# Padding the on-chip tiles of a four-layer decoder trunk so that matmul operands begin at multiples of 128 bytes

## The chip, the cores and the metric

The kernel runs on one core of one Trainium2 chip. The metric is device time in microseconds, the median of several runs. The profile is of one execution on that core, taken by the hardware profiler.

## What is computed

The reference is a small decoder trunk on 512 tokens of width 1024 in float32, with two layers. Each layer adds to the residual stream x: half a SwiGLU block, a token mixer, and half a second SwiGLU block, each behind an RMS norm.

```python
for layer in range(DEPTH):                      # 2
    x = x + 0.5 * _swiglu(_rmsnorm(x, g[0]), w_gate0, w_up0, w_down0)
    h = _rmsnorm(x, g[1])
    mix = _conv_rwkv_mixer(h, ...) if layer % 2 == 0 else _mla_mixer(h, ...)
    x = x + mix
    x = x + 0.5 * _swiglu(_rmsnorm(x, g[2]), w_gate1, w_up1, w_down1)

def _swiglu(h, w_gate, w_up, w_down):           # 1024 -> 2816 -> 1024
    return (jax.nn.silu(h @ w_gate) * (h @ w_up)) @ w_down
```

So there are four SwiGLU blocks. The mixer of layer 0 is a gated short convolution beside an RWKV-7 recurrence, that of layer 1 latent attention with 8 heads. Most of the arithmetic is in the four SwiGLU blocks.

## The kernel before

Activations are kept transposed: channels on the 128 partitions, the 512 tokens along the free axis, so x is eight tiles x0 to x7 of 128x512 float32. Products in float32 are made from two halves: a value is split into a rounded part ("h", type fp32r) and what is left ("l"), and the helper `mm3` (L98 to L102) issues three matmuls into one PSUM tile: weight-h by x-h (L100), weight-h by x-l (L101), weight-l by x-h (L102). In each the x operand is streamed (512 columns), and a 128x128 block of weights is loaded ahead of it as the stationary operand.

`weight` (L64) brings 128x512 float32 of weights by one DMA into a ring of four raw tiles (wr), ACT makes the rounded half (wh, L71), DVE or GpSimd the rest (wl, L72), in rings of four each. `gemm_steps` (L82) walks the contraction in blocks of 128 and calls mm3 for each.

`ffn` (L158) is one SwiGLU block. For each of 22 column blocks it accumulates a gate tile pg and an up tile pu over the eight x tiles (48 matmuls: three into pg, three into pu, and so on): this is called the gate/up phase here, 22 x 48 = 1056 matmuls. DVE and ACT make the activation of each block in temporary tiles and split it into ah and al, which stay on chip. Then for each of eight output blocks po is accumulated over the 22 ah/al tiles: the down phase, 8 x 66 = 528 matmuls. In both phases TensorE takes its instructions in the order written; other engines follow through semaphores that the framework sets.

The layers between use the same mm3 for their larger products (pp and po in layer 0; po in layer 1). Layer 1 has more split products written out in place: pab (L400 to L402, 384 and 320 columns), pq and pk (L556 to L558, 384 and 512 columns; here the weights are streamed and the tile ch or cl of a token block is stationary), the scores ps (L603 to L607, key tiles kh and kl streamed, query tiles stationary) and attention times values (L642 to L644). L608 adds the mask to the scores by a short bf16 matmul.

Where a tile lies: each pool gives its tiles consecutive places in every partition, each rounded up to 32 bytes, and a pool begins where the one opened before it ends. The first tile of the kernel lies at a multiple of 128. From the sizes in the code this gives, modulo 128 bytes:

```
tiles                                   before           after
raw and split weights wr, wh, wl          96               0
x, split x (xh, xl), oh, ol               96               0
temporary tiles, six buffers      96,0,32,64,96,0          0
ah, al                                    32               0
layer 0: large tiles (mb, b, ar, ma)       0               0
layer 0: tiles of g()              0, 32, 64, 96           0
layer 1: split input weights wih, wil     96               0
layer 1: ch, cl of token block 0..3   0,32,64,64     64,96,0,0
layer 1: q, k, v of head pairs 0, 2       96               0
layer 1: q, k, v of head pairs 1, 3        0               0
layer 1: th, tl                            0               0
```

The columns of a weight tile that one matmul loads begin a multiple of 512 bytes further in; only the first two projections of layer 0, with 64 and 96 columns a block, step by 256 and 384 bytes.

Of the kernel before, what the change touches and what calls it, by code (L numbers as in the profile page):

```python
# [8 lines left out]
F32 = mybir.dt.float32  # L9
# [8 lines left out]
WCOL = 512  # L18
NRAW = 4
NSPLIT = 4  # L20


class Lazy:
    def __init__(self, make):
        self.make = make
# [5 lines left out]
class Trunk:  # L31
    def __init__(self, tc, d, stack):
        self.tc, self.nc, self.d = tc, tc.nc, d
        nc = self.nc
        open_ = lambda **k: stack.enter_context(tc.tile_pool(**k))
        self.cp = open_(name="const", bufs=1)
        self.wp = open_(name="w", bufs=3)
        self.xp = open_(name="xs", bufs=1)
        self.tp = open_(name="tmp", bufs=6)
        self.mm = open_(name="mm", bufs=4, space=PSUM)  # L40
        self.sm = open_(name="sm", bufs=4, space=PSUM)
        self.n = 0
        self.filler = iter(())
        self.x = [self.xp.tile([128, T], F32, name=f"x{k}") for k in range(KD)]
        self.xh = self.xl = None
        self.gains = self.cp.tile([128, 6, KD], F32, name="gains")
        nc.sync.dma_start(self.gains, d["gains"])
        self.loaded = 0
        self.load(0)
        self.ones = self.cp.tile([128, 128], F32, name="ones")  # L50
        nc.vector.memset(self.ones, 1.0)
        self.eps = self.cp.tile([128, 1], F32, name="eps")
        nc.vector.memset(self.eps, 1e-6)
        warm = self.cp.tile([128, 1], F32, name="warm")
        nc.scalar.activation(warm, self.eps, AF.Silu)

    def uid(self, s):
        self.n += 1
        return f"{s}_{self.n}"

    def t(self, name, n=T, dt=F32, p=128):
        return self.tp.tile([128, 520], dt, name=self.uid(name), tag="t")[0:p, 0:n]

    def weight(self, src, cols, scale=None, lo_on=None):  # L64
        nc = self.nc
        raw = self.wp.tile([128, WCOL], F32, name=self.uid("wr"), tag="wr", bufs=NRAW)[:, 0:cols]
        hi = self.wp.tile([128, WCOL], F32R, name=self.uid("wh"), tag="wh", bufs=NSPLIT)[:, 0:cols]
        lo = self.wp.tile([128, WCOL], F32R, name=self.uid("wl"), tag="wl", bufs=NSPLIT)[:, 0:cols]
        nc.sync.dma_start(raw, src)
# [10 lines left out]
            pass  # L80

    def gemm_steps(self, outs, nk, m, xh, xl, lo_on=None):  # L82
        """outs: [(psum, weight block [128, nk * m])]; contraction over nk tiles of x."""
        step = min(nk, WCOL // m)
        for k0 in range(0, nk, step):
            k1 = min(nk, k0 + step)
            w = [self.weight(src[:, k0 * m : k1 * m], (k1 - k0) * m, lo_on=lo_on) for _, src in outs]
            for k in range(k0, k1):
                s = slice((k - k0) * m, (k - k0 + 1) * m)
                for (ps, _), (wh, wl) in zip(outs, w):  # L90
                    self.mm3(ps, wh[:, s], wl[:, s], xh[k], xl[k], k == 0, k == nk - 1)
                    yield
# [109 lines left out]
class Mla(Trunk):  # L202
# [136 lines left out]

    def qkv(self, pool):  # L340
        t = lambda n, a, b: pool.tile([128, a, b], F32R, name=self.uid(n), tag=n)
        sq = pool.tile([128, 8], F32, name=self.uid("sq"), tag="sq")
        return t("qh", 4, T), t("ql", 2, T), t("kh", 4, T), t("kl", 4, T), t("vh", 4, 256), t("vl", 4, 256), sq

    def mla_out(self, hp):
# [15 lines left out]
    def mla_in(self, iw, q0):  # L361
        nc, d = self.nc, self.d
        self.win = []
        for k in range(KD):
            h = iw.tile([128, 704], F32R, name=f"wih{k}")
            l = iw.tile([128, 704], F32R, name=f"wil{k}")
            for c in (slice(0, 384), slice(384, 704)):
                raw = self.wp.tile([128, WCOL], F32, name=self.uid("wr"), tag="wr", bufs=NRAW)[:, 0 : c.stop - c.start]
                nc.sync.dma_start(raw, d["w_oi"][k][:, c])
                nc.scalar.activation(h[:, c], raw, AF.Copy)  # L370
                (nc.vector if k % 2 == 0 else nc.gpsimd).tensor_tensor(l[:, c], raw, h[:, c], op=ALU.subtract)
            self.win.append((h, l))
        self.rt = self.mp.tile([128, 4], F32, name="rt")
        self.ch, self.cl, self.kr, self.kb = [], [], [], []
        self.cur, self.pab = self.qkv(q0), {}
        proj = self.mla_proj(0, self.cur)
        self.in_mm((0, 1))
        post = [self.in_post(iw, 0)]
        for tb in range(1, 4):
            if tb > 1:  # L380
                self.in_mm((tb,))
            post.append(self.in_post(iw, tb))
            self.in_t(post.pop(0))
            if tb >= 2:
                for _ in range(2):
                    next(proj)
        self.in_t(post.pop(0))
        return proj
# [260 lines left out]


DECAY = float(np.exp(-0.5))
# columns of the per-channel parameter block
MU_R, MU_K, MU_V, MU_L, MU_G, W0, A0, KK, KA, RK, LNW, LNB, CW = 0, 4, 8, 12, 13, 14, 18, 22, 26, 30, 34, 38, 42
NEV = 54
G = 520
LORA_FILL = 1
DECAY_FILL = 1
KEYS_FILL = 3
# [9 lines left out]
class Even(Mla):  # L668
# [26 lines left out]
    def g(self, tag, n=T, p=128, dt=F32):  # L695
        bufs = 3 if tag == "c" else 1
        return self.gp.tile([128, G], dt, name=self.uid(tag), tag=tag, bufs=bufs)[0:p, 0:n]

    def even_setup(self):
        nc, d, rp = self.nc, self.d, self.rp  # L700
        self.ev = rp.tile([128, NEV], F32, name="ev")
        nc.sync.dma_start(self.ev, d["ev"])
        self.om = rp.tile([128, 14], F32, name="om")
        nc.vector.tensor_scalar(self.om, self.ev[:, 0:14], -1.0, 1.0, op0=ALU.mult, op1=ALU.add)
        self.oka = rp.tile([128, 8], F32, name="oka")
        nc.vector.tensor_scalar(self.oka[:, 0:4], self.ev[:, KA : KA + 4], -1.0, None, op0=ALU.mult)
        nc.vector.tensor_scalar(self.oka[:, 4:8], self.ev[:, KA : KA + 4], 1.0, -1.0, op0=ALU.mult, op1=ALU.add)
        self.mask = rp.tile([128, 128], F32, name="emask")
        nc.sync.dma_start(self.mask, d["emask"])
        self.bones = rp.tile([128, 128], F32, name="bones")  # L710
        nc.sync.dma_start(self.bones, d["bones"])
        self.zero = rp.tile([128, 64], F32, name="zero")
        nc.gpsimd.memset(self.zero, 0.0)
        self.gneps = rp.tile([128, 1], F32, name="gneps")
        nc.vector.memset(self.gneps, 64e-5)
# [383 lines left out]
def lay_mla(inp,o):  # L1099
    a={k:np.asarray(v) for k,v in inp.items()}  # L1100
    c=np.ascontiguousarray
    o["ident"]=np.eye(128,dtype=np.float32)
    o["mask"]=np.triu(np.full((128,128),-1e30,np.float32),1)
    o["pos"]=c(a["positions"].reshape(4,128).T)
    fr=(10000.0**(-np.arange(0,64,2)/64)).astype(np.float32)
    o["freq"]=c(np.broadcast_to(fr.astype(np.float32),(128,32)))
    qn,kn=a["mla_q_norm"][0],a["mla_k_norm"][0]
    o["nope_g"]=c(np.broadcast_to(np.concatenate([qn[:128],kn[:128]]),(128,256)))
    o["rope_g"]=c(np.broadcast_to(np.concatenate([qn[128:],kn[128:]]),(128,128)))
    o["mla_v"]=c(np.concatenate([a["mla_q_a_norm"][0].reshape(3,128).T,a["mla_kv_a_norm"][0].reshape(2,128).T],1))  # L1110
    o["w_oi"]=c(a["odd_w_in"][0].reshape(8,128,704))
    w=a["mla_w_kv_up"][0].reshape(2,128,4,2,2,128)  # k p hp h (kn|v) d
    o["w_kv"]=c(w.transpose(2,1,0,4,3,5).reshape(4,128,1024))
    i=np.arange(192)
    w=a["mla_w_q_up"][0].reshape(3,128,4,384)[...,np.concatenate([i,192+(i+128)%192])]
    o["w_q"]=c(w.transpose(2,1,0,3).reshape(4,128,1152))
    w=a["odd_w_out"][0].reshape(4,2,128,8,128)  # hp c p m d
    o["w_oo"]=c(w.transpose(0,2,3,1,4).reshape(4,128,2048))
    return o

def lay_even(inp,o):
    a={k:np.asarray(v) for k,v in inp.items()}
    c=np.ascontiguousarray
    w=a["even_w_in"][0]  # [1024, 3232]: b 512 | c 512 | h 512 | r k v 512 | dw 32 da 32 dg 96
    rk=1536
    blocks=[w[:, rk+1536:rk+1600], w[:, rk+1600:rk+1696]]
    rwkv=lambda i,j: w[:, rk+i*512+j*128:rk+i*512+j*128+128]
# [3 lines left out]
    for j in range(4):  # L1131
        s=slice(j*128,j*128+128)
        b,cc,h=(w[:,i*512:i*512+512][:,s] for i in range(3))
# [4 lines left out]
    pad=lambda v:np.concatenate([v,np.zeros(128-len(v),np.float32)])[:,None]  # L1138
# [14 lines left out]
def layout(inp):  # L1153
    return lay_even(inp, lay_mla(inp, lay(inp)))
# [33 lines left out]
```

## Time and profile before

| what | value |
|---|---|
| median of 3 runs | 2049.99 us (2046.57 to 2051.52) |
| span of the profiled execution, from the first to the last instruction | 2044.8 us |
| the profiled execution's own time beside its span | not listed; the runs' times are 1.8 to 6.7 us over this span |
| TensorE busy | 96% of the span, 10030 matmuls |
| VectorE, ScalarE, GpSimd busy | 53%, 38%, 15% |
| DMA engines, mean busy share | 28%, 85 GB/s |
| gate/up phases | about 25 to 254, 734 to 962, 1097 to 1326, 1689 to 1918 us |
| down phases | 254 to 377, 962 to 1086, 1326 to 1449, 1918 to 2041 us |
| layer 0 mixer, layer 1 mixer | 377 to 717 us, 1449 to 1677 us |

How to read it: PE is the matmul part of TensorE, PEld its weight loads, which overlap the matmuls. Matmuls are pipelined: the start of the next comes before the end of the one before, so the durations of single matmuls overlap and their sum is more than the span. What a matmul costs in a long row of them is the distance from start to start, which can be had from a count in a stretch, or from first and last start of a group. [...]

### The profile page before, as it was taken

The numbers are of one execution on the slowest core, as the hardware profiler recorded it, in microseconds if no ns is written. First come the engines' busy times: TensorE is split into PE (matmuls) and PEld (weight loads), VectorE is DVE, ScalarE is ACT, GpSimd is POOL, SyncE is SP. The second block draws the span as 40 slices with busy tenths as digits, with TensorE's granted clock in tenths as the row PEclk, the third lists the DMA queues.
The fourth block names the chain that finished last, engine by engine and source line by source line (L and its number), as shares of the span: only waits on it lengthen the run. The fifth ranks groups of instructions, "written<-read, shape, count | busy, mean of one in ns | idle before, by whom it ended". The sixth has DMA issues, their size and how long they took to land.

```text
span 2044.8 us, 26989 instructions
## 1 busy us (share of the span) xinstructions
PE 1964.4 (96%) x10030; PEld 1590.4 (78%) x10030; DVE 1080.7 (53%) x1914; ACT 771.5 (38%) x1497; POOL 298.6 (15%) x342
## 2 busy tenths in 40 slices
PE   8999999967999999999999999999988999999999
PEld 6888888746776778888888888888877778888887
DVE  6444433499954864444335444433377775444422
ACT  5333332533422443333233333333475544333221
POOL 2000000266333410000000000000353430000000
PEclk9999999988999999999999999999998999999999
DMA  4333333221111123323332332333311123333332
GB/s 144 97 97 99 91 101 92 82 63 52 46 38 53 61 93 96 101 93 101 91 95 95 94 102 93 96 98 94 95 36 33 42 68 103 94 103 93 103 109 78
DMA packets 99892, 174.47 MB, mean 85 GB/s; under 512 B 11792, under 2 KB 20496, under 8 KB 99760
## 3 DMA queue, kind: packets, MB, share of 16 engines
q1 hardware_dynamic: 99760, 172.74, 28.1%
q8 instruction: 79, 1.29, 0.3%
q14 instruction: 53, 0.43, 0.1%
HBM read 170.60 MB, written 2.10 MB: 84 GB/s over the span
## 4 chain that ended last, share of the span: by engine, by line
PE 64%; DVE 8%; issue 3%; POOL 2%; ACT 1%; DMA 1%; POOLq 0%; SPq 0%; ACTq 0%; DVEq 0%
PE po L100 7%; PE po L101 7%; PE po L102 7%; PE pu L100 6%; PE pg L100 6%; PE pu L102 6%; PE pg L101 6%; PE pu L101 6%; PE pg L102 6%; PE pp L100 1%; PE pp L101 1%; PE pp L102 1%; PE s L907 0%; POOL s L493 0%; DVE pr L932 0%
## 5 line engine op out<-in xcount | busy, mean ns | idle before, releaser
L71 ACT ACTIVATE wh<-wr 128x512 fp32r<-128x512 f32 (+2 forms) x647 | 399.2, 619 | 919.5 <-PE pg L101 452.9
L72 DVE TENSOR_TENSOR wl<-wr,wh 128x512 fp32r<-128x512 f32 (+2 forms) x567 | 383.2, 679 | 428.0 <-ACT wh L71 427.5
L100 PE MATMUL pg<-xh,wh 128*128 128x512 f32 x704 | 277.2, 394 | 6.6 <-ACT wh L71 6.0
L100 PE MATMUL pu<-xh,wh 128*128 128x512 f32 x704 | 275.2, 391 | 3.2 <-DVE x L1085 2.6
L101 PE MATMUL pg<-xl,wh 128*128 128x512 f32 x704 | 275.5, 391 | 2.3 <-DVE xl L118 2.3
L102 PE MATMUL po<-ah,wl 128*128 128x512 f32 x704 | 277.4, 394 | 0.0
L100 PE MATMUL po<-ah,wh 128*128 128x512 f32 x704 | 277.4, 394 | 0.0
L101 PE MATMUL po<-al,wh 128*128 128x512 f32 x704 | 277.4, 394 | 0.0
L102 PE MATMUL pg<-xh,wl 128*128 128x512 f32 x704 | 275.0, 391 | 0.0
L102 PE MATMUL pu<-xh,wl 128*128 128x512 f32 x704 | 274.9, 391 | 0.0
L101 PE MATMUL pu<-xl,wh 128*128 128x512 f32 x704 | 274.8, 390 | 0.0
L173 DVE TENSOR_TENSOR g<-pg,rinv 128x512 f32<-128x512 f32 x88 | 60.9, 692 | 286.9 <-PE pg L102 286.5
L137 POOL TENSOR_TENSOR acc<-acc,sq 128x512 f32<-128x512 f32 x42 | 57.1, 1360 | 1061.6 <-ACT sq L136 1061.3
L100 PEld LDWEIGHTS pg<-xh,wh 128*128 128x128 f32 x704 | 132.8, 189 | 35.7 <-ACT wh L71 6.0
L100 PEld LDWEIGHTS pu<-xh,wh 128*128 128x128 f32 x704 | 132.7, 189 | 32.1 <-ACT sin L282 2.9
L101 PEld LDWEIGHTS pg<-xl,wh 128*128 128x128 f32 x704 | 132.9, 189 | 31.9 <-DVE xl L118 3.7
L102 PEld LDWEIGHTS po<-ah,wl 128*128 128x128 f32 x704 | 131.6, 187 | 32.7
L100 PEld LDWEIGHTS po<-ah,wh 128*128 128x128 f32 x704 | 131.7, 187 | 32.6
L101 PEld LDWEIGHTS po<-al,wh 128*128 128x128 f32 x704 | 131.7, 187 | 32.5
L102 PEld LDWEIGHTS pu<-xh,wl 128*128 128x128 f32 x704 | 132.6, 188 | 28.1 <-DVE wl L72 0.5
L102 PEld LDWEIGHTS pg<-xh,wl 128*128 128x128 f32 x704 | 132.8, 189 | 27.8 <-DVE wl L72 0.5
L101 PEld LDWEIGHTS pu<-xl,wh 128*128 128x128 f32 x704 | 132.7, 189 | 27.4
(365 smaller groups left out, 2633.8 us busy)
## 6 DMA issues: line engine op xcount, KB each, us to landing
wr<-in_wg SPq DMA_DIRECT2D x176, 256.0 KB, 2.6
wr<-in_wu SPq DMA_DIRECT2D x176, 256.0 KB, 2.9
wr<-in_wd SPq DMA_DIRECT2D x160, 256.0 KB, 2.7
wr<-in_w_ei SPq DMA_DIRECT2D x49, 256.0 KB, 2.7
wr<-in_wd SPq DMA_DIRECT2D x32, 128.0 KB, 2.1
wr<-in_w_eo SPq DMA_DIRECT2D x16, 256.0 KB, 2.7
wr<-in_w_oo SPq DMA_DIRECT2D x16, 256.0 KB, 3.1
wr<-in_w_q SPq DMA_DIRECT2D x12, 192.0 KB, 2.4
```

Of the source, the lines that this page charges most:

```text
L71: nc.scalar.activation(hi, raw, AF.Copy)
L72: (lo_on or nc.vector).tensor_tensor(lo, raw, hi, op=ALU.subtract)
L100: nc.tensor.matmul(ps, wh, xh, start=first, stop=False)
L101: nc.tensor.matmul(ps, wh, xl, start=False, stop=False)
L102: nc.tensor.matmul(ps, wl, xh, start=False, stop=last)
L137: nc.gpsimd.tensor_tensor(acc, acc, sq, op=ALU.add)
L173: nc.vector.tensor_tensor(g, pg, rinv, op=ALU.mult)
```

## The change

No instruction is added, removed or moved. Six tiles get longer or a tile that nobody uses is put behind others, so that what is allocated after them shifts: 32 bytes behind the constants (all later pools), the temporary tiles from 520 to 544 floats, the tiles of `g` in layer 0 from 520 to 544, the parameter block `ev` from 54 to 64 floats, `sq` from 8 and `rt` from 4 to 32 floats in layer 1. The column "after" in the table above is the outcome. The rest of the diff takes out comments.

```diff
+CONST_PAD = 8
+TMP = 544
@@ class Trunk: __init__
         nc.scalar.activation(warm, self.eps, AF.Silu)
+        self.cp.tile([128, CONST_PAD], F32, name="pad")
@@ def t
-        return self.tp.tile([128, 520], dt, name=self.uid(name), tag="t")[0:p, 0:n]
+        return self.tp.tile([128, TMP], dt, name=self.uid(name), tag="t")[0:p, 0:n]
@@ def qkv
-        sq = pool.tile([128, 8], F32, name=self.uid("sq"), tag="sq")
+        sq = pool.tile([128, 32], F32, name=self.uid("sq"), tag="sq")
@@ def mla_in
-        self.rt = self.mp.tile([128, 4], F32, name="rt")
+        self.rt = self.mp.tile([128, 32], F32, name="rt")[:, 0:4]
@@
-G = 520
+G = 544
@@ def even_setup
-        self.ev = rp.tile([128, NEV], F32, name="ev")
+        self.ev = rp.tile([128, NEV + 10], F32, name="ev")[:, 0:NEV]
```

## Rows read from the trace of the kernel before

**Rows 1.** The page's busy times: engine, busy us (share of the span), instructions.
```profile
PE 1964.4 (96%) x10030; PEld 1590.4 (78%) x10030; DVE 1080.7 (53%) x1914; ACT 771.5 (38%) x1497; POOL 298.6 (15%) x342
```
**Rows 2.** The page's chain of waits, shares of the span by line.
```profile
PE po L100 7%; PE po L101 7%; PE po L102 7%; PE pu L100 6%; PE pg L100 6%; PE pu L102 6%; PE pg L101 6%; PE pu L101 6%; PE pg L102 6%; PE pp L100 1%; PE pp L101 1%; PE pp L102 1%; PE s L907 0%; POOL s L493 0%; DVE pr L932 0%
```
**Rows 3.** Stretches of 100 us: us, PE busy (matmuls), granted clock, DMA share, GB/s.
```profile
100.00:200.00 100.00, 100.00 (x443) 1.00 0.31 95
260.00:360.00 100.00, 100.00 (x430) 1.00 0.34 94
...
1720.00:1820.00 100.00, 100.00 (x443) 1.00 0.31 95
1930.00:2030.00 100.00, 100.00 (x431) 1.00 0.37 107
```
**Rows 4.** Tile pu, second gate/up phase: duration ns min/median/max, first and last start.
```profile
L100 PEld LDWEIGHTS pu<-xh,wh x168: 187/188/188, 734.4 to 961.5; 128*128 128x128 f32 x168
L100 PE MATMUL pu<-xh,wh x168: 389/389/389, 734.6 to 961.7; 128*128 128x512 f32 x168
```
**Rows 5.** Tile po in the second down phase, the same columns.
```profile
L100 PE MATMUL po<-ah,wh x176: 394/394/394, 962.4 to 1084.9; 128*128 128x512 f32 x176
L101 PEld LDWEIGHTS po<-al,wh x176: 187/187/188, 962.4 to 1084.9; 128*128 128x128 f32 x176
```
**Rows 6.** Timeline of TensorE, up-projection of token block 1: start us, us, instruction.
```profile
1550.09 0.39 PE L556 MATMUL pk<-wh,ch 128*128 128x512 f32 x1
...
1551.25 0.39 PE L558 MATMUL pk<-wh,cl 128*128 128x512 f32 x1
```
**Rows 7.** The same view, scores of head pairs 1 and 3.
```profile
1557.10 0.39 PE L604 MATMUL ps<-kl,qh 128*128 128x512 f32 x1
...
1558.03 0.23 PE L608 MATMUL ps<-maskb,identb 128*128 128x128 bf16 x1
...
1632.29 0.39 PE L603 MATMUL ps<-kh,qh 128*128 128x512 f32 x1
...
1633.22 0.40 PE L607 MATMUL ps<-kl,qh 128*128 128x512 f32 x1
```
**Rows 8.** The same view, scores of head pair 2.
```profile
1596.75 0.39 PE L604 MATMUL ps<-kl,qh 128*128 128x512 f32 x1
...
1597.68 0.23 PE L608 MATMUL ps<-maskb,identb 128*128 128x128 bf16 x1
```
**Rows 9.** A stretch at half clock, its window row and timeline.
```profile
1575.57:1577.20 1.63, 1.63 (x5) 0.50 0.10 38
...
1575.57 0.63 PE L604 MATMUL ps<-kl,qh 128*128 128x512 f32 x1
...
1576.85 0.63 PE L607 MATMUL ps<-kl,qh 128*128 128x512 f32 x1
```
**Rows 10.** Groups of TensorE instructions by line: busy us, mean ns, idle before.
```profile
L100 PE MATMUL pp<-xh,wh 128*128 128x512 f32 (+2 forms) x208 | 87.2, 419 | 1.4 <-ACT wh L71 1.4
L402 PE MATMUL pab<-wil,xh 128*128 128x384 f32 x64 | 21.0, 330 | 0.2 <-POOL wil L371 0.2
```
**Rows 11.** Tile g, second gate/up phase: duration ns min/median/max, first and last start.
```profile
L173 DVE TENSOR_TENSOR g<-pg,rinv x22: 691/692/693, 738.8 to 961.9; 128x512 f32<-128x512 f32 x22
```
**Rows 12.** First down phase, groups by line; then the page's DMA issues, us to landing.
```profile
L72 DVE TENSOR_TENSOR wl<-wr,wh 128x512 fp32r<-128x512 f32 x32 | 22.1, 691 | 51.4 <-ACT wh L71 51.4
L71 ACT ACTIVATE wh<-wr 128x512 fp32r<-128x512 f32 x32 | 20.2, 633 | 53.0 <-PE po L101 49.1 <-ACT sq L136 3.2 <-ACT acc L133 0.6
...
wr<-in_wd SPq DMA_DIRECT2D x160, 256.0 KB, 2.7
```
**Rows 13.** Timeline of TensorE, the 64- and 96-column projections of layer 0.
```profile
380.13 0.40 PE L100 MATMUL pp<-xh,wh 128*64 128x512 f32 x1
...
382.66 0.39 PE L102 MATMUL pp<-xh,wl 128*64 128x512 f32 x1
...
384.21 0.40 PE L102 MATMUL pp<-xh,wl 128*96 128x512 f32 x1
...
386.31 0.39 PE L102 MATMUL pp<-xh,wl 128*96 128x512 f32 x1
```

## The prediction

> **What bounds the kernel now.** I read the busy table first: TensorE is busy 96% of the span [rows 1]. The chain of waits agrees: its longest links are the three multiply lines of the helper mm3 for po, pg and pu, 6 to 7% of the span each, thus nine groups with about 58% [rows 2]. So the next view is stretches inside the feed-forward phases: I looked at eight of 100 us, one in each gate/up and each down phase; the first and last pairs are shown. The reader is to see three things in them: TensorE 100 us busy of 100, the granted clock 1.00, and yet two different counts, 443 matmuls in a gate/up stretch and 430 or 431 in a down stretch, of the same 128x512 shape [rows 3].
>
> The two counts are two paces. In the second gate/up phase the L100 matmuls into pu start from 734.6 to 961.7 us, 168 of them, with six matmuls from each to the next: 227.1 / (167 x 6) = 226.7 ns from start to start [rows 4]. In the down phase behind it 176 start from 962.4 to 1084.9, three matmuls apart: 122.5 / (175 x 3) = 233.3 ns [rows 5]. The weight load beside them takes the same in both (188 and 187 ns), so it doesn't set the difference. Four blocks x 22 x 8 x 2 x 3 = 4224 gate/up matmuls at 226.7 are 957.5 us, 4 x 8 x 22 x 3 = 2112 down matmuls at 233.3 are 492.8 us: 1450 us, 71% of the span, in which nothing but this pace counts.
>
> **What the change does to a matmul.** It moves tiles only. From the sizes in the code I take two offsets of every matmul, modulo 128: that of the streamed operand and that of the weights. Before, gate/up has 96 and 96 (distance 0), down has 32 and 96 (distance 64). After, both have 0 and 0.
>
> Does the distance matter, or the offset itself? The trace has other pairs, in the attention layer. The key/value up-projection of token block 1 streams weights at 96 against stationary tiles at 32, distance 64 again, although here it is the stationary operand that lies at 32: five intervals from 1550.09 to 1551.25 us, 232 ns each, like the down phase [rows 6]. The score matmuls of the odd head pairs have both operands at 0, those of the even pairs both at 96. From L604 to L608 the first take 1557.10 to 1558.03, the second 1596.75 to 1597.68: four intervals of 232.5 ns in both, and another run at 0 gives the same, 1632.29 to 1633.22 [rows 7, 8]. So offset 0 by itself buys nothing there; and in short runs also distance 0 isn't at 226.7. I read 226.7 as a pace into which a long undisturbed run at distance 0 settles, and 233.3 as that of distance 64.
>
> **The sum.** Gate/up keeps distance 0: 4224 x 0 = 0. Down goes from distance 64 to 0, and I take 226.7 for it, the row of the same shape and length that is nearest: 2112 x (233.33 - 226.67) = 2112 x 6.67 ns = 14.1 us, all on the path, as TensorE has no idle time in the down stretch. [...]
>
> The other products of split operands, about 1700 with 320 to 512 columns, in the even and the attention layer, change distances in both directions (the up-projections' stationary tiles go from 0, 32, 64, 64 to 64, 96, 0, 0). By the same step of 6.67 ns they could give or cost 11 us if every one moved; their lines hold some hundred matmuls each [rows 10], they are interrupted often, and I take 0.
>
> Vector engines: the six temporary buffers lie at four different offsets (96, 0, 32, 64, 96, 0) and the DVE multiply into them runs from 691 to 693 ns over all of them [rows 11]. So DVE and ACT get 0. Transfers: the padding shifts the landing address of weight tiles from 96 to 0 too. In a down phase one 256 KB transfer feeds 12 matmuls, 2.8 us, and lands after 2.7 us with four buffers in the ring; its split takes 633 ns on ACT and 691 on DVE [rows 12]. A faster down phase asks for one each 2.72 us; with a DMA share of 0.34 to 0.37 [rows 3] the ring covers that. Without cover a late tile would show as a wait of TensorE; there is none of note in these phases now.
>
> Sum: 2044.8 - 14.1 = 2030.7 us of span. The median of the runs, 2049.99, lies 5.2 us over the profiled span (the three runs 1.8 to 6.7), so 2036 us.
>
> [...] The rows show 226.7 and 233.3 ns for one shape beside equal weight loads [rows 4, 5]. [...]
>
> **Rivals.**
> 1. *Down stays at its pace.* 2050 us. Either the cause isn't the offset (the down phase also streams from higher tiles), or the distance counts over more than 128 bytes: by the sizes in the code the new ah tiles lie 256 bytes from the weights modulo 512, while gate/up lies at 0 modulo 512 before and after. For it: the 96-column projection, whose weight slices step by 384 bytes at distance 0 modulo 128, takes 2.10 us for nine intervals, 233.3 ns; the 64-column one (steps of 256 bytes) 2.53 us for eleven, 230.0 [rows 13]. Against it: in both the distance modulo 512 changes after each three matmuls and fewer weight columns are loaded; no long run with a constant 256 is in the trace. At 230.0 for down it would be 2112 x 3.3 = 7.0 us less, 2043.
> 2. *Gate/up loses its good pace: slower.* Its place is the 4224 matmuls. At 0/0 the trace has 232.5 ns and nowhere 226.7 [rows 7]. If that is what 0/0 gives, gate/up costs 4224 x 5.8 = 24.5 us more, against 14.1 or less gained in down: 2060 to 2074. It decides from 230.0 on: a gate/up pace 3.3 ns longer eats the whole gain. Against it: at 96/96 the same short chain runs at 232.5 too [rows 8], and 96/96 settles in long runs.
> [...]
>
> **How the numbers follow.** Forecast (down settles at 226.7, gate/up unchanged) 0.43, by itself 2031 to 2041 with 5 us for the short products and the spread of the runs; rival 1 0.29, of which 0.06 at 230; rival 2 0.17; rival 3 0.11. About 0.3%, 6 us, can be told from no change. Faster: 0.40 + 0.06 + 0.11, less a little for part gains, 0.55. Slower: rival 2, 0.17. Same: 0.28. The range, 2024 to 2066, has the forecast, rival 1 and the lower part of rival 2; it leaves out rival 3 and the upper half of rival 2, together about 0.2.
>
> **What would show it.** Right: a down stretch of 100 us holds 443 matmuls, its L100 starts lie 0.680 us apart, the phase is 119.7 instead of 123.2 us, gate/up stretches hold 443 still, and the weight loads stay at 187. Wrong by rival 1: 430 in down. By rival 2: under 436 in gate/up. [...] The prediction as a whole would be wrong if the even and attention layers (377 to 717 and 1449 to 1677 us) changed by more than the feed-forward phases do.

## The result, and the profile after

The changed kernel takes 2033.4 us (median of 4 runs, 2030.9 to 2035.3), against 2048.7 for the kernel before beside it: ratio 0.9924, interval 0.991 to 0.9938, thus 13 to 18 us less. Forecast were 14.1 us less, and 2036.

The page after, its span and busy times; they answer to [rows 1].
```profile
span 2032.8 us, 26989 instructions
...
PE 1953.0 (96%) x10030; PEld 1593.5 (78%) x10030; DVE 1083.8 (53%) x1914; ACT 771.1 (38%) x1497; POOL 297.9 (15%) x342
```
TensorE still works 96% of a shorter span, with the same number of matmuls: it was relieved neither of matmuls nor of waiting, and yet it is busy for 11.4 us less, so some of its matmuls follow each other faster. Which ones, the stretches show; those of after answer to [rows 3], again gate/up, down, gate/up, down, with TensorE's busy time (matmuls), granted clock (as a share of full speed), DMA share and GB/s.
```profile
100.00:200.00 100.00, 100.00 (x443) 1.00 0.29 95
260.00:360.00 100.00, 100.00 (x443) 1.00 0.34 96
1720.00:1820.00 100.00, 100.00 (x443) 1.00 0.31 100
1930.00:2025.00 95.00, 95.00 (x421) 1.00 0.34 102
```
Gate/up has its 443 matmuls as before. A down stretch, 430 before, now has 443 too (421 in 95 us is the same pace). From first and last start, after, second gate/up and second down phase, to be laid beside [rows 4, 5]:
```profile
L103 PEld LDWEIGHTS pu<-xh,wh x168: 187/188/188, 733.1 to 960.3; 128*128 128x128 f32 x168
L103 PE MATMUL pu<-xh,wh x168: 389/389/397, 733.3 to 960.5; 128*128 128x512 f32 x168
...
L103 PE MATMUL po<-ah,wh x176: 389/389/390, 961.2 to 1080.2; 128*128 128x512 f32 x176
L104 PEld LDWEIGHTS po<-al,wh x176: 187/188/188, 961.2 to 1080.2; 128*128 128x128 f32 x176
```
(L103 and L104 are L100 and L101 of before.) Gate/up: 227.2 / (167 x 6) = 226.7 ns. Down: 119.0 / (175 x 3) = 226.7 ns, where [rows 5] had 233.3. The weight loads keep their 187 to 188 ns. The modelled duration of a down matmul fell only from 394 to 389 ns; the start-to-start distance is what shows the 6.7.

The second down phase, from its first matmul to the first of the next gate/up phase, is 119.6 us (961.2 to 1080.8) after 123.2 before (962.4 to 1085.6); four of them give 14 us. The vector engines are as they were: the DVE multiply into the temporary tiles, [rows 11] before, is on the same 692 ns with all of them at multiples of 128:
```profile
L176 DVE TENSOR_TENSOR g<-pg,rinv x22: 691/692/694, 737.5 to 960.7; 128x512 f32<-128x512 f32 x22
```
The profiled span fell by 12.0 us, less than the medians. By the starts of its phases layer 0 took 343 us in that profile against 340 before (373.0 to 716.3, 377.4 to 717.5). In the profiles of the experiments below layer 0 lies between 340 and 343, and it takes 340 in the run with ah at distance 128, which has all of the padding, so this is scatter between single profiles and not a cost of the padding.

### The profile page after: what moved, and what is told of

Read it like the earlier page. It is cut to its first block, busy times and chain, and to the rows that moved or that the text cites. A ratio compares the mean times of both kernels' runs of the same rounds, so it can differ in the third digit from the quotient of the medians.

```text
span 2032.8 us, 26989 instructions
## 1 busy us (share of the span) xinstructions
PE 1953.0 (96%) x10030; PEld 1593.5 (78%) x10030; DVE 1083.8 (53%) x1914; ACT 771.1 (38%) x1497; POOL 297.9 (15%) x342
## 4 chain that ended last, share of the span: by engine, by line
PE 65%; DVE 9%; issue 2%; POOL 2%; ACT 2%; DMA 1%; POOLq 0%; ACTq 0%; DVEq 0%
PE po L103 7%; PE po L104 7%; PE po L105 7%; PE pu L103 6%; PE pu L104 6%; PE pu L105 6%; PE pg L104 6%; PE pg L103 6%; PE pg L105 6%; PE pp L103 1%; PE pp L104 1%; PE pp L105 1%; PE s L910 0%; DVE pr L935 0%; DVE ma L942 0%
## 5 line engine op out<-in xcount | busy, mean ns | idle before, releaser
L103 PE MATMUL pg<-xh,wh 128*128 128x512 f32 x704 | 276.8, 393 | 6.7 <-ACT wh L74 6.0
L103 PE MATMUL pu<-xh,wh 128*128 128x512 f32 x704 | 275.3, 391 | 3.3 <-DVE x L1088 2.6
L104 PE MATMUL pg<-xl,wh 128*128 128x512 f32 x704 | 275.5, 391 | 1.8 <-DVE xl L121 1.7
L104 PE MATMUL pu<-xl,wh 128*128 128x512 f32 x704 | 274.8, 390 | 0.0
L103 PE MATMUL po<-ah,wh 128*128 128x512 f32 x704 | 273.9, 389 | 0.0
L104 PE MATMUL po<-al,wh 128*128 128x512 f32 x704 | 273.9, 389 | 0.0
L103 PEld LDWEIGHTS pg<-xh,wh 128*128 128x128 f32 x704 | 132.7, 188 | 35.3 <-ACT wh L74 6.0
L104 PEld LDWEIGHTS pg<-xl,wh 128*128 128x128 f32 x704 | 132.7, 188 | 32.2 <-DVE xl L121 4.1
L103 PEld LDWEIGHTS pu<-xh,wh 128*128 128x128 f32 x704 | 132.6, 188 | 32.1 <-ACT sin L285 2.9
L104 PEld LDWEIGHTS pu<-xl,wh 128*128 128x128 f32 x704 | 132.7, 189 | 27.5
L104 PEld LDWEIGHTS po<-al,wh 128*128 128x128 f32 x704 | 132.1, 188 | 27.6
L103 PEld LDWEIGHTS po<-ah,wh 128*128 128x128 f32 x704 | 132.1, 188 | 27.2
```

What stands on the lines that cost most here:

```text
L103: nc.tensor.matmul(ps, wh, xh, start=first, stop=False)
L104: nc.tensor.matmul(ps, wh, xl, start=False, stop=False)
```

## The experiments

In all of them only places of tiles differ, as before. The ratios are to the kernel before, run beside each group of experiments (2047.5 to 2048.7 us); differences to the changed kernel are between medians of different groups, so 1 us more or less means nothing in them. "Distance" is the offset of the streamed operand less that of the weights. Where a mean pace is given with two decimals, it is the mean from start to start over the 2112 down or 4224 gate/up matmuls of the profile, without the few gaps of over 245 ns; it is read from the starts in the trace, to the nanosecond. Each fence shows stretches of TensorE: us, busy (matmuls), granted clock, DMA share, GB/s.

### Boundaries or distance: only the temporary tiles padded

```diff
 kernel before
-        return self.tp.tile([128, 520], dt, ...
+        return self.tp.tile([128, 544], dt, ...
```


> Kernel before with the temporary tiles at 544 floats and nothing else of the change: weights and x stay at 96 modulo 128, ah and al move from 32 to 96, so the distance of streamed operand and weights is 0 in both phases and no operand is on a boundary. Theory D (only the distance counts): down pace 226.7 instead of 233.3 ns, 100 us of it hold 443 matmuls, gate/up unchanged, 14.1 us less than before (ratio 0.993). Theory B (both operands have to begin at multiples of 128): no operand does, down stays at 233.3 and 430 in 100 us, ratio 1.000.

Measured: 2034.6 us, ratio 0.9935 (0.992 to 0.995). Gate/up, then down:
```profile
100.00:200.00 100.00, 100.00 (x443) 1.00 0.29 95
260.00:360.00 100.00, 100.00 (x443) 1.00 0.34 95
```
Weights, x, ah and al all lie at 96 modulo 128, and the whole gain is there. So beginning at multiples of 128 is not what the gain comes from: theory B falls. The rest of the padding (constants, layer 0, `sq`, `rt`) adds nothing that can be told: 2034.6 and 2033.4, with overlapping intervals.

### Only the constants padded

```diff
 kernel before
         nc.scalar.activation(warm, self.eps, AF.Silu)
+        self.cp.tile([128, 8], F32, name="pad")
```


> Kernel before with the 32 bytes behind the constants and nothing else: weights and x at 0, ah and al at 64, distance 64 in down and 0 in gate/up. Theory D: down 233.3, gate/up 226.7, ratio 1.000. Theory B: down not on a boundary of 128, the same 1.000. Theory C (a multiple of 64 is enough for each operand): down 226.7, 14.1 us less, ratio 0.993.

Measured: 2048.1 us, ratio 1.0001 (0.9991 to 1.001).
```profile
100.00:200.00 100.00, 100.00 (x443) 1.00 0.28 95
260.00:360.00 100.00, 100.00 (x430) 1.00 0.34 94
```
Weights and x on boundaries, ah at 64: the paces of before, to the count. Theory C falls, and gate/up is no faster at 0/0 than at 96/96.

### x moved instead of ah

```diff
 changed kernel
+        self.xp.tile([128, 16], F32, name="xpad")
         self.x = [self.xp.tile([128, T], F32, ...
         self.xh = self.xl = None
+        self.tp.tile([128, 16], F32, name="tpad", bufs=1)
```


> Changed kernel with 64 bytes ahead of the x tiles and 64 more behind them: x, xh and xl at 64 against weights at 0, ah and al at 0 again. Theory D: gate/up goes to 233.3 ns (430 in 100 us), 4224 x 6.67 = 28.2 us more than the changed kernel, 14.1 more than before (ratio 1.007 to before), down stays at 226.7. Theory C (multiples of 64 suffice): as the changed kernel, ratio 0.993. A third one, that the difference belongs to the down phase (its place or its tiles) and not to offsets: gate/up stays at 226.7, ratio 0.993.

Measured: 2054.7 us, ratio 1.003 (1.0018 to 1.0042).
```profile
100.00:200.00 100.00, 100.00 (x439) 1.00 0.29 95
260.00:360.00 100.00, 100.00 (x432) 1.00 0.34 95
```
A miss for every theory as it stood. Gate/up did get slower by moving x alone, so the difference doesn't belong to the down phase; but its mean is 228.93 ns, not 233.3. And down, whose operands all begin at multiples of 128, is at 232.39, not 226.7. Worked out from the two paces: 4224 x 2.26 + 2112 x 5.72 = 21.6 us over the changed kernel, 2055, which is the measured time. What differs in down from the changed kernel is the distance over a longer period: 384 bytes modulo 512 here, 256 there. From here on the theory was one of the distance modulo 256 (F): 0 fast, 64 a little slower, 128 and 192 slow.

### ah at distance 32

```diff
 changed kernel
         self.xh = self.xl = None
+        self.tp.tile([128, 8], F32, name="tpad", bufs=1)
```


> Changed kernel with 32 bytes more behind the x tiles: ah and al at 32, weights at 0, distance 32. Theory D in the form that only distance 0 is fast: down near 233 ns as the up-projection chains at distance 32 (232 to 235), 14 us over the changed kernel, ratio 1.000 to before. D in the form that only distance 64 is slow: 226.7, ratio 0.993. A pace between the two, as 230.0, would give 7 us, ratio 0.996.

Measured: 2047.8 us, ratio 1.0001 (0.9991 to 1.001); down 233.34 ns.
```profile
100.00:200.00 100.00, 100.00 (x443) 1.00 0.29 95
260.00:360.00 100.00, 100.00 (x431) 1.00 0.33 93
```
32 bytes take the whole gain away.

### All on multiples of 128, distance 128

```diff
+        self.tp.tile([128, 32], F32, name="tpad", bufs=1)
```
(the changed kernel with this line where the one above stands; the same place in the next ones)

> Changed kernel with 128 bytes more behind the x tiles: everything still begins at multiples of 128, but the distance of ah and al to the weights is 128 modulo 256 instead of 0. Theory F (the pace is a function of the distance modulo 256; from the run with x at 64 the value at 128 is 232.4 ns): down 232.4, 2112 x 5.7 = 12 us over the changed kernel, ratio 0.999 to before. Theory D (distance modulo 128; the 232.4 there came from the gate/up pattern in which that run entered the down phase): 226.7, ratio 0.993.

Measured: 2048.5 us, ratio 1.0 (0.9989 to 1.001); down 233.32 ns.
```profile
100.00:200.00 100.00, 100.00 (x443) 1.00 0.30 95
260.00:360.00 100.00, 100.00 (x430) 1.00 0.34 94
```
This is the run that decides against the change's own description: every operand that it aligned still begins at a multiple of 128, and nothing is left of the gain. Theory D, that of the prediction, falls with it; the distance counts over 256 bytes. (The pace is 233.3 rather than the 232.4 of the run with x at 64, where ah, al and the weights lie at the same places. What differs there is x and with it the pace of the gate/up phase that comes before; that the entry into the phase is worth the 1 ns was not tested.)

### The other side: distance 64, in down

```diff
+        self.tp.tile([128, 16], F32, name="tpad", bufs=1)
```


> Changed kernel with 64 bytes more behind the x tiles: ah and al 64 from the weights modulo 256, on the side opposite to the kernel before (192). Theory F: 228.9 ns as gate/up at 64 in the run with x at 64, 2112 x 2.2 = 4.7 us over the changed kernel, ratio 0.995. Theory D (64 and 192 are the same modulo 128): 233.3, 14.1 us over, ratio 1.000. If gate/up's own pattern of two PSUM tiles made the 228.9: 233.3 too.

Measured: 2040.0 us, ratio 0.9962 (0.9947 to 0.9977); down 228.92 ns.
```profile
100.00:200.00 100.00, 100.00 (x442) 1.00 0.30 95
260.00:360.00 100.00, 100.00 (x439) 1.00 0.34 94
```
64 gives 228.9 in down as it did in gate/up (by the sizes 320 modulo 512 here and 64 there), while the 192 of the kernel before gives 233.3. The two are the same modulo 128, so this is a second witness against theory D. It is worth 4.8 us over the changed kernel by the pace, and 6.5 by the medians.

### Distance 192 in gate/up

```diff
+        self.xp.tile([128, 48], F32, name="xpad")
         self.x = [self.xp.tile([128, T], F32, ...
         self.xh = self.xl = None
+        self.tp.tile([128, 16], F32, name="tpad", bufs=1)
```


> Changed kernel with 192 bytes ahead of the x tiles and 64 more behind them: gate/up at distance 192, that of the down phase of the kernel before, and ah and al at distance 0. Theory F: gate/up 233.3 ns, 28.2 us over the changed kernel, 14.1 over before (ratio 1.007); down 226.7. Theory D: the distance is 64 modulo 128, and gate/up 228.9 as in the run with x at 64: 9.4 us over the changed kernel, ratio 0.997. If the offset mattered only in down: ratio 0.993.

Measured: 2061.7 us, ratio 1.0057 (1.004 to 1.0075); gate/up 233.33 ns, down 226.70.
```profile
100.00:200.00 100.00, 100.00 (x430) 1.00 0.31 95
260.00:360.00 100.00, 100.00 (x442) 1.00 0.36 98
```
The roles are exchanged: the distance of the old down phase put into gate/up costs 28.3 us over the changed kernel (28.2 expected), and down at distance 0 (modulo 512 as well) has the same pace as at 256. It is the same step of 6.67 ns, in the other phase, with the other sign, on twice the matmuls.

This run also has what [rows 9] could not give, half-clock matmuls at a slow distance, early in the second gate/up phase (a stretch, then starts in it):
```profile
726.50:728.60 2.10, 2.10 (x6) 0.50 0.40 133
...
726.52 0.63 PE L105 MATMUL pg<-xh,wh 128*128 128x512 f32 x1
...
728.65 0.63 PE L107 MATMUL pu<-xh,wl 128*128 128x512 f32 x1
```
Five intervals take 2.13 us, 426 to 427 ns each as in [rows 9], whose operands are at distance 0: at granted clock 0.50 the distance costs nothing that can be seen.

### Distances 96, 160 and 224

```diff
+        self.tp.tile([128, 24], F32, name="tpad", bufs=1)   # 96; 40 for 160, 56 for 224
```


> Changed kernel with 96 bytes more behind the x tiles: ah and al 96 from the weights. No row has a long run at 96; the up-projection chains at 96 modulo 128 ran at about 231 ns. Theory F gives a pace between those of 64 and 128, 228.9 to 232.4, so 5 to 12 us over the changed kernel, ratio 0.995 to 0.999. Theory D with only 0 fast: 231 to 233.

> Changed kernel with 160 bytes more behind the x tiles: ah and al 160 from the weights modulo 256. Theory F (a function of the distance modulo 256, so far 226.7 at 0, 228.9 at 64 and 233.3 at 32, 96, 128 and 192): 233.3, the pace of all distances but 0 and 64, ratio 1.000 to before. If the function is symmetric (160 as 96): 233.3 as well. If a second good distance lies here: under 230, ratio under 0.997.

> Changed kernel with 224 bytes more behind the x tiles: ah and al 224 from the weights, 32 below the next multiple of 256. Theory F symmetric around 0: 233.3 as at 32, ratio 1.000. If what lies just below a multiple of 256 acts as the multiple: 226.7, ratio 0.993.

Measured: 2047.4 us, ratio 0.9998 (0.9986 to 1.0009); 2051.3, 1.0019 (1.0009 to 1.003); 2047.3, 0.9998 (0.9988 to 1.0009). Down paces 233.36, 234.27 and 233.34 ns. The down stretch of each:
```profile
260.00:360.00 100.00, 100.00 (x430) 1.00 0.34 94
```
```profile
260.00:360.00 100.00, 100.00 (x429) 1.00 0.33 93
```
```profile
260.00:360.00 100.00, 100.00 (x431) 1.00 0.33 93
```
96 missed the guess of a smooth curve between 64 and 128. There is no second good distance in steps of 32; 160 is the worst.

### Distance 16

```diff
-                h = ap.tile([128, T], F32R, name=f"ah{j}_{m}")
-                l = ap.tile([128, T], F32R, name=f"al{j}_{m}")
+                hl = ap.tile([128, 2 * T + 64], F32R, name=f"ahl{j}_{m}")
+                h, l = hl[:, 4 : T + 4], hl[:, T + 4 : 2 * T + 4]
```


> Changed kernel with each ah and al pair in one tile, read from 16 bytes past a multiple of 256: distance 16, no operand of the down phase at a multiple of 32. If the pace counts distances in steps of 32 bytes: 226.7, ratio 0.993. If each byte counts: between 226.7 and the 233.3 at 32, so 0 to 14 us over the changed kernel, ratio 0.993 to 1.000.

Measured: 2038.6 us, ratio 0.9962 (0.9949 to 0.9975); down 231.66 ns.
```profile
100.00:200.00 100.00, 100.00 (x443) 1.00 0.29 95
260.00:360.00 100.00, 100.00 (x434) 1.00 0.33 94
```
16 bytes cost 5.0 ns of the 6.67: even less than one step of 32 counts. By the pace the run should be 10.5 us over the changed kernel, 2044, and it is 5 us better. In the profiled run, most of it shows at the head of the second gate/up phase. The waits of TensorE from 700 to 735 us and the stretch from 712 us, changed kernel first:
```profile
PE pu L103 <- DVE x L1088: 2.6, 1, 2.6
PE pg L103 <- DVE x L1088: 0.7, 1, 0.7
...
712.00:735.00 23.00, 19.74 (x78) 0.93 0.28 96
```
```profile
712.00:735.00 23.00, 23.00 (x101) 1.00 0.31 103
```
In the changed kernel (and in the one before) the new phase waits some 3 us for layer 0's last additions to x (2.6 + 0.7 us, before 2.6 + 0.6) and then has 3.4 us at granted clock 0.50 (719.8 to 723.2, before 722.0 to 725.4); in this run there is no wait there and the clock stays at 1.00: 23 matmuls more in 23 us, worth 5.2 us at 226.7. The first 48 matmuls of this phase take 16 us in the kernel before and in the changed kernel; at the pace of this run's stretch, 101 in 23 us, 48 take 11. Whether the other tile sizes of ah and al bring this about was not tried; it is a side effect of its own, and the 2038.6 say little about 16 bytes. The pace does.

### The short products of layer 1 at distance 0 too

```diff
 changed kernel
-TMP = 544
+TMP = 520
...
+        self.tp.tile([128, 16], F32, name="tpad", bufs=1)
...
-        sq = pool.tile([128, 32], F32, ...
+        sq = pool.tile([128, 64], F32, ...
-        self.rt = self.mp.tile([128, 32], F32, name="rt")[:, 0:4]
+        self.rt = self.mp.tile([128, 64], F32, name="rt")[:, 0:4]
-        b_ = self.mp.tile([128, 1], F32, name=f"kb{tb}")
+        b_ = self.mp.tile([128, 64], F32, name=f"kb{tb}")[:, 0:1]
```


> Changed kernel with the small tiles of layer 1 padded to 256 bytes (and the temporary tiles at 520 floats with 64 bytes beside them), so that the split products of layer 1 have distance 0 modulo 256 too, which pab (128), pk and pq (0 to 96) don't have in the changed kernel. Theory F: layer 1's chains are short, 336 matmuls that could save some 3 ns each, 1 us: 2032 us, not to be told from the changed kernel. If short chains settle as soon as all distances are 0: 231.6 to 226.7 for pk and 175 to 170 for pq, 1.5 us, layer 1 at 225 instead of 227 us. If small tiles at 256 bytes cost something: layer 1 longer.

Measured: 2032.5 us, ratio 0.9925 (0.9908 to 0.9941): the changed kernel's time. Mean intervals within the chains, without those over 245 ns (512 columns) or 208 ns (384): pk 230.3 ns (231.6 in the changed kernel), pq 174.6 (175.1), pab with 384 columns 175.6 (176.1), from some 60 to 100 intervals each. The differences are of about 1 ns or less, and pk stays 3.6 ns above the 226.7 of a long run: short chains don't get that pace from the distance alone, as forecast. Layer 1 took 229.6 us in this profile against 227.0, with a granted clock of 0.96 against 0.98 over it; as it lies between 226.6 and 230.0 in the other profiles, this is neither a gain nor a cost.

## Why the prediction was right, and where it was not

The distance modulo 256 and the pace of a long run, all of 128x512 matmuls at granted clock 1.00:

```
distance   0      16     32     64     96     128    160    192    224
ns       226.7  231.7  233.3  228.9  233.4  233.3  234.3  233.3  233.3
```
(128 has 232.4 in the run with x at 64.) The values at 0, 64 and 192 were had in both phases, and at 0 and 64 with distances that differ modulo 512; 16, 32, 96, 160 and 224 come from one run each.

*What bounds the kernel.* Right: the four down phases fell by 14 us, which lies within the 13 to 18 us of the runs, as TensorE had no idle time in them, and no wait took its place: the down stretch is still busy for 100 us of 100, so the transfers followed at the shorter pace.

*That the distance matters, not the offset.* Right, and shown from both sides: at 96/96/96 the whole gain (2034.6), at multiples of 128 throughout none (2048.5).

*That the distance counts modulo 128.* Wrong. This premise stood under the term of 2112 x 6.67 ns and under rival 1. [rows 6] could not show it, since its distance of 64 modulo 128 is 192 modulo 256, that of the old down phase, and the prediction took the agreement for proof of the shorter period. The term came out by luck, because the new distance is 256, a whole period. Had the temporary tiles ended 128 bytes later, the same words would have described a change worth nothing.

*The size.* 14.1 us forecast; 14 us by the down phases; 15.3 by the medians (13 to 18). The 5.2 us that the sum adds to the span are no cost beside it: each run that lists both is 2 us over its own span, and the rest is that the profiled execution of the kernel before was one of the quicker ones.

*Gate/up and the mixers at 0.* Right. 443 in each stretch; the intervals of the short products (pk, pq, pab) changed by about 1 ns.

*The rivals.* Rival 1 (down stays) didn't come. Its second form, a longer period, was right in kind: the period is 256, not 512. The rows that spoke for it [rows 13] have distances 0, 128 and 256 mixed, so part of what looked like a period of 512 was one of 256; the 64-column projection, at distance 0 modulo 256 all the time, runs at 230.0 before and after, and that stays unexplained. Rival 2: gate/up at 0/0 keeps 226.7, so the 232.5 of [rows 7, 8] belong to their short chains and not to 0/0. Rival 3, which has 0.11 in the sum for "faster", rests on a pace below 226.7 for both phases, a term that no run shows: nothing went below 226.7 at any distance.

*Whether something else makes the step.* A long run of matmuls is here 2 to 8 ns slower each by where the streamed operand lies relative to the weights (228.9 ns at 64, 234.3 at 160, against 226.7 at 0): for this type and shape the two operands' places act on the pace together. An obvious rival, that the slow matmuls collide with other traffic (DMAs, ACT and DVE write into the weight pool, whose tiles share one offset in all runs), is ruled out by the end of the last down phase of the kernel before. Nothing but TensorE works there any more: us, then busy time of PE, PEld, DVE, ACT and POOL, granted clock, DMA share, GB/s.
```profile
2037.00:2040.60 3.60, 3.60 (x17) 2.90 (x16) 0.00 (x0) 0.00 (x0) 0.00 (x0) 1.00 0.00 0
...
2037.19 0.39 PE L102 MATMUL po<-ah,wl 128*128 128x512 f32 x1
...
2039.99 0.39 PE L102 MATMUL po<-ah,wl 128*128 128x512 f32 x1
```
The twelve intervals between these starts are 233.3 ns each, as in the whole phase. Besides the matmuls only the weight loads are busy in that stretch (2.90 us, 16 of them). They keep a median of 187 or 188 ns in the down phases of the kernel before, of the changed kernel and of the runs at 16, 64, 128 and 160, but at 160 some of them get longer, up to 193, where in the changed kernel none takes over 188:
```profile
L104 PEld LDWEIGHTS po<-ah,wh x176: 187/188/193, 964.0 to 1087.0; 128*128 128x128 f32 x176
```
By what means the two act on each other, no run shows. That the period is 256 bytes, that 64 is the next best distance and that 16 already costs most of the step is measured; a picture of the memory that gives all three was not found. Nor is it known why a matmul at distance 0 takes 226.7 ns at granted clock 1.00, 13 ns more than half of the 427 ns that [rows 9] have at 0.50.

## What to carry to other kernels

In long unbroken runs of fp32r matmuls at granted clock 1.00 (here 512 columns, 128x128 weights) compare start-to-start paces of phases of one shape: a difference of some 3% at equal clock without waits (here 233.3 against 226.7 ns) can be the place of the tiles. Bring the streamed operand and the weights to the same offset modulo 256 bytes; a multiple of 128 for each was here neither needed (443 down matmuls in 100 us with all at 96 modulo 128) nor enough (430 at distance 128). One tile a few bytes longer, far from the matmuls, can make or lose it (32 bytes behind x: 226.7 to 233.3 ns), so read the distance from the pools after each change of a tile's size.

## What the runs showed of the hardware that was not expected

- The pace depends on the distance modulo 256 bytes (226.7 ns at 0 and 256, 233.3 at 128), and not evenly: 64 costs 2.2 ns of 226.7, its mirror 192 costs 6.7.
- A run at a slow distance needn't be even. Starts in the down phase at distance 128 (start us, duration, instruction):
```profile
299.73 0.40 PE L104 MATMUL po<-ah,wh 128*128 128x512 f32 x1
299.97 0.39 PE L105 MATMUL po<-al,wh 128*128 128x512 f32 x1
300.20 0.40 PE L106 MATMUL po<-ah,wl 128*128 128x512 f32 x1
300.43 0.39 PE L104 MATMUL po<-ah,wh 128*128 128x512 f32 x1
300.66 0.40 PE L105 MATMUL po<-al,wh 128*128 128x512 f32 x1
300.90 0.39 PE L106 MATMUL po<-ah,wl 128*128 128x512 f32 x1
```
  To the nanosecond these intervals alternate between 237 or 238 and 229, with a mean of 233.3; at 96 they repeat 231, 238, 231, at 64 226, 229, 232. In the down phases of the changed kernel (226 or 227 ns, one of 2108 at 228) and of the kernel before (233 or 234) they are alike within 1 ns, so an even pace is no sign of a good distance, and a single interval says little about a pace.
- The extra time that the distance costs was seen at granted clock 1.00 alone (6.67 ns at 192): at 0.50 the same matmul takes 426 to 427 ns at distance 0 ([rows 9], and 722.28 to 724.84 us in gate/up of the kernel before, six intervals) and at 192 (the run with 192 in gate/up).
